# Two of the seven Strassen-Winograd products share one PSUM bank, in both MLP stages of a recurrent decoder layer

## The chip, the core and the metric

The kernel runs on one NeuronCore of a Trainium2 chip. Five engines each run their own instruction stream in order: TensorE (PE, matmuls, with its weight loads shown apart as PEld), VectorE (DVE), ScalarE (ACT), GpSimd (POOL) and SyncE (SP, which here issues most DMA transfers). They wait for each other through semaphores. Matmuls write PSUM, which is divided into banks; DVE and ACT read the sums from there. The metric is the device time of one execution in microseconds (us). The clock granted to TensorE is 2.4 GHz or 1.2 GHz; the profile gives it as a share of full speed.

## What is computed

One inference step of one layer with 2048 prompt tokens and 32 sample tokens (T = 2080). A recurrent mixer comes first and is not touched. What the change touches is the MLP at the end, float32 throughout:

```
h = x * (1.0 + sc2) + sh2
f = jnp.dot(jnp.square(jax.nn.relu(jnp.dot(h, p['mlp_w1']) + p['mlp_b1'])), p['mlp_w2']) + p['mlp_b2']
x = layer_norm(ALPHA * x + g2 * f, p['ln2_g'], p['ln2_b'])
```

`mlp_w1` is 1024 x 4096 and `mlp_w2` 4096 x 1024.

## The kernel before

**Groups and chunks.** The 2080 tokens go through the MLP in three groups, 0, 1 and 2, of 696, 692 and 692 columns (`groups`). A group is two halves of `w` = 348 or 346 columns. Within a group the 4096 hidden features are walked in 16 chunks of 256 (`c`, 0 to 15; 14 in group 2, whose last two chunks take another path). For each chunk `mlp1` makes 256 hidden features for all columns of the group. After four chunks `mlp2_seven` multiplies them by their rows of `mlp_w2` and adds the result to the SBUF tile `acc`. So a group is four times: four calls of `mlp1`, one of `mlp2_seven`.

**Seven products.** Each of these matrix products is cut into 2 x 2 blocks and done with seven block products in Winograd's form instead of eight. With the left operand's combinations a11, a12, a22, s1 to s4 and the right one's b11, b21, b22, t1 to t4:

```
X  = a11*b11            C11 = X + a12*b21
X += s2*t2  (U2)        C12 = U2 + s1*t1 + s4*b22
X += s3*t3  (U3)        C22 = U3 + s1*t1
X += a22*t4             C21 = X
```

s1*t1 is the P5 and s4*b22 the P3 of the title. X is a running sum that stays in one PSUM bank ("the X bank") while a11, s2, s3 and a22 add to it; between two of them an engine reads the bank, and the next product's first matmul has to wait for that read. A product in `mlp1` is 12 matmuls (4 blocks of the contraction, 3 each, since a float32 operand is split in a high and a low part, tiles named h... and l...). In `mlp2_seven` it is 48 matmuls over four banks, two of everything because four chunks make two pairs.

**mlp1 before.** `prod` runs one product, into a new bank from `rot(M1_BANKS, ...)` or onto the one it is given. The reads: s1 <- X after a11 (ACT copy), u2 <- X after s2 (ACT copy), u2 <- X after s3 (ACT copy), and Relu of X after a22 (ACT). The bank of s1*t1, `p5_s`, is read twice by DVE: u4 = p5_s + u2 (U2 + P5), and `put(1, 1, p5_s, u2)` after s3. The product s4 has a bank of its own, which `put(0, 1, ps, u4)` reads. `put` is a DVE instruction that adds bank, bias and an SBUF tile, and then the squared ReLU. Chunk 0 of groups 1 and 2 has an order of its own.

**mlp2_seven before.** `PRODUCTS` lists left operand, right operand, whether the product adds to the X banks, and to which quarters of `acc` its banks are then added. DVE does the adding (`add(V, dst, ps[b], dst)`), ACT a copy where the quarter is still empty. Products not in X take fresh banks from `rot("CD")`.

**Order and weights.** The program is written chunk by chunk, but the compiler's scheduler decides how the instructions of neighbouring chunks interleave on each engine; each engine then runs its list in order. Group 0 makes the combinations of the weights itself (DVE, ACT, POOL), uses them and stores them to `W1d` and `W2d` in HBM. Groups 1 and 2 load them from there, one 512 KB tile for each 12 matmuls, through SP's queue, in the order in which the program names them (`order_of` for mlp1, `PRODUCTS` for mlp2), into 15 slots that are reused in turn (`kept`, `READY`): the load of a tile waits until the tile 15 places earlier has been used.

Matmul results carry the names m1... for `mlp1` and m2... for `mlp2_seven`: the X bank of `mlp1` is m1a11_group_chunk, P5's is m1s1_group_chunk.

Of the kernel before, what the change touches and what calls it, by code (L numbers as in the profile page):

```python
# [12 lines left out]
AF = mybir.ActivationFunctionType  # L13
# [4 lines left out]
P = 128  # L18
# [17 lines left out]
def trunk(ctx: ExitStack, tc: tile.TileContext, *args):  # L36
# [324 lines left out]
    with lpool("ab") as ab:  # L361
# [95 lines left out]
        for nm, rows in (("A", rowsA), ("B", rowsB)):  # L457
            n = sum(r for _, r in rows)
            rt = ab.tile([P, 4, 288], F32, tag="hf", name="rt" + nm, bufs=2)[:, 0, 0:P]
            o = 0  # L460
# [316 lines left out]

    def order_of(gidx, c):

        if c:  # L780
            return "a11", "a12", "s2", "s1", "s3", "s4", "a22"
        return ("a11", "a12", "s4", "s2", "s1", "s3", "a22") if gidx else ("a11", "s2", "s1", "s3", "a22", "a12", "s4")

    def weights(gidx, c):

# [259 lines left out]
    with lpool("p5") as p5_:  # L1045
# [2 lines left out]

        acc = p5_.tile([P, 4, 4, HW], F32, tag="acc", name="acc")

        PRODUCTS = (("a11", "b11", True, (0,)), ("s1", "t1", False, (2, 3)), ("a12", "b21", False, (0,)),
                    ("s2", "t2", True, (2,)), ("s4", "b22", False, (2,)), ("s3", "t3", True, (3,)),
                    ("a22", "t4", True, (1,)))

        def block(q):
            return acc[:, 2 * q:2 * q + 2].rearrange("p a j t -> p (a j) t")
# [1 line left out]
        def mlp1(gidx, c, wts=None):  # L1058
            g0, npr, w = groups[gidx]
            ops = wts or weights(gidx, c)  # L1060
            nm = f"{gidx}_{c}"
            hid = [p5_.tile([P, 2, HW], F32, tag="hid", name=f"hid{q}_{nm}", bufs=8) for q in range(2)]
            hid = [t[:, :, :w] for t in hid]

            def prod(key, rt, o, on=None):

                ps = rot(M1_BANKS, f"m1{key}_{nm}")[:, :w] if on is None else on
                wh, wl = ops[key]
                hh, hl = h2[rt]
                for k in range(4):  # L1070
                    for i, (x, h) in enumerate(((wh, hh), (wh, hl), (wl, hh))):
                        PE.matmul(ps, x[:, k, :], h[:, k, o:o + w], start=(on is None and k + i == 0),  # L1072
                                  stop=(k == 3 and i == 2), skip_group_check=on is not None)
                return ps

            def vt(v):
                return p5r.tile([P, HW], F32, tag="v", name=f"{v}_{nm}", bufs=3)[:, :w]

            def bias(f):
                return vec["mlp_b1"][:, 2 * c + f:2 * c + f + 1]  # L1080

            def square(v, on_act=False):
                if on_act:
                    act(v, v, AF.Relu)
                    act(v, v, AF.Square)
                else:
                    stt(v, v, 0.0, v, ALU.max, ALU.mult)

            def put(f, q, ps, s):
                v = hid[q][:, f, :]  # L1090
                stt(v, ps, bias(f), s, ALU.add, ALU.add)
                square(v, SQA[2 * f + q])

            s1, u2, u4 = vt("s1"), vt("u2"), vt("u4")
            v01, v10 = hid[1][:, 0, :], hid[0][:, 1, :]
            x = p5_s = None
            for key in order_of(gidx, c):
                if key == "a11":
                    x = prod(key, "b1", 0)
                    act(s1, x, AF.Copy)  # L1100
                elif key == "a12":
                    put(0, 0, prod(key, "b2", 0), s1)
                elif key == "s2":
                    prod(key, "t42", w, x)
                    act(u2, x, AF.Copy)
                elif key == "s1":
                    p5_s = prod(key, "t13", 0)
                    add(V, u4, p5_s, u2)
                    if gidx and not c:
                        add(V, v01, v01, u4)  # L1110
                        square(v01, SQA[1])
                elif key == "s3":
                    prod(key, "t13", w, x)
                    act(u2, x, AF.Copy)
                    put(1, 1, p5_s, u2)
                elif key == "s4":
                    ps = prod(key, "b2", w)
                    if gidx and not c:
                        act(v01, ps, AF.Identity, bias=bias(0))
                    else:  # L1120
                        put(0, 1, ps, u4)
                else:
                    prod(key, "t42", 0, x)
                    act(v10, x, AF.Relu, bias=bias(1))
                    act(v10, v10, AF.Square)
            return hid
# [12 lines left out]
        def mlp2_seven(gidx, c0, hids, steps=None):  # L1139
# [44 lines left out]
                        tail(bv, "t4", "b21", "b21", "t2")  # L1184

            taken = [c0 > 0] * 4
            banks = None
            for l, r, grows, to in PRODUCTS:
                rs = []
                for nm, av, bv in pairs:  # L1190
                    prepare(l, nm, av, bv)
                    rs.append(part(f"{r}_{nm}", bv[r]))
                fresh = not (grows and banks)
                if not grows:
                    ps = [rot(M2_BANKS, f"m2{l}_{gidx}_{c0}_{b}")[:, :w] for b in range(4)]
                else:
                    if fresh:
                        banks = [ptile([P, 512], X_BANKS[b], f"m2x_{gidx}_{c0}_{b}")[:, :w] for b in range(4)]
                    ps = banks
                for s_ in range(2):  # L1200
                    for n, ((nm, av, bv), (hh, hl)) in enumerate(zip(pairs, rs)):
                        at = W2d[c0 // 2 + n, KEYS.index(l), s_]
# [139 lines left out]
        BEH = ("s4", "t3", "t4")  # L1342
        SQA = (0, 1, 1, 1)
        PB = 3
        M1_BANKS, M2_BANKS, X_BANKS = "ADB", "CD", "ABAB"
        LATE = range(2, 14, 2)
        STAGE = range(4, 12)
        epst = sel[:, 0, 0:1]
# [537 lines left out]
```

## Time and profile before

| what | value |
|---|---|
| median of 3 runs (lowest, highest) | 2162.76 us (2157.93, 2165.63) |
| the profiled execution, its own time | 2165.93 us |
| its span, first to last instruction | 2164.1 us |
| PE busy / DVE busy / ACT busy | 2038.4 / 1426.8 / 1006.3 us |
| mean granted clock of TensorE | 0.978 |

The profiled execution is 1.8 us longer than its span. The MLP begins near 735 us of the span; group 0 fills most of 780 to 1300 us, groups 1 and 2 follow up to about 2115 us, and the rest is the end of the last layer norm. A share of busy time is an average over these stages, which have different limits, so the rows below are taken stage by stage.

### The profile page before, as it was taken

To read this page: it belongs to the slowest core of one execution; us is meant where nothing else is said; L and a number is where in the kernel's file an instruction comes from. 1 tells how busy PE (TensorE), PEld (TensorE's weight loads), DVE (VectorE), ACT (ScalarE), POOL (GpSimd) and SP (SyncE) were. 2 spreads that over 40 slices of the span, in tenths; PEclk is the share of its full clock that TensorE was granted. 3 is DMA by queue.
4 is the path that set the end of the run, shared out by engine and by line. 5 is a ranking of instruction groups with operands and counts; after the bars stand their busy time and mean duration, and the time that the engine had idled before them with its cause. 6 is when DMAs were issued, how large, how long until landed. Compare 5 with 4: busy or idle time off the path is not lost.

```text
span 2164.1 us, 35479 instructions
## 1 busy us (share of the span) xinstructions
PE 2038.4 (94%) x13055; PEld 1915.4 (89%) x13055; DVE 1426.8 (66%) x2766; ACT 1006.3 (47%) x1923; POOL 489.7 (23%) x327
## 2 busy tenths in 40 slices
PE   7998999989999989889899899999999999999996
PEld 4987888888877789888899889999999999999996
DVE  5677897467887898688797854445444444554476
ACT  3446665546676456554645534333334343333342
POOL 2245323432433322121222401000002000001003
PEclk9999999999999989999999999999999999999998
DMA  9799765453342598999989899888889988898871
GB/s 334 162 267 266 220 192 171 134 149 83 103 110 79 181 325 315 397 341 369 348 325 351 312 365 370 306 282 297 304 293 332 383 302 303 286 310 293 278 271 53
DMA packets 367596, 571.39 MB, mean 264 GB/s; under 512 B 129451, under 2 KB 250703, under 8 KB 367423
## 3 DMA queue, kind: packets, MB, share of 16 engines
q1 hardware_dynamic: 363975, 567.84, 76.8%
q8 instruction: 103, 1.69, 0.3%
q10 hardware_dynamic: 3448, 1.29, 0.2%
q14 instruction: 70, 0.57, 0.1%
HBM read 388.10 MB, written 180.94 MB: 263 GB/s over the span
## 4 chain that ended last, share of the span: by engine, by line
PE 43%; DVE 4%; issue 3%; DMA 2%; POOL 0%; ACT 0%; SPq 0%; POOLq 0%; DVEq 0%; ACTq 0%
PE m1a L1072 15%; PE m2x L1211 11%; PE m1s L1072 6%; PE m2s L1211 6%; PE m2a L1211 3%; PE lt L1297 1%; DVE hw2s L44 1%; DVE acc L44 1%; DMA W1d<-w1s 0%; PE m L1247 0%; PE m L1248 0%; PE m L1249 0%; DVE hid L44 0%; DMA n<-Nd 0%; DVE lb L44 0%
## 5 line engine op out<-in xcount | busy, mean ns | idle before, releaser
L44 POOL TENSOR_TENSOR y<-y,ln_g 128x512 f32<-128x512 f32 (+3 forms) x28 | 37.6, 1360 | 636.7 <-ACT y L65 463.3
L65 ACT ACTIVATE ht<-hid 128x692 fp32r<-128x692 f32 (+1 forms) x92 | 72.1, 783 | 174.1 <-PE m2s L1211 62.8
L65 ACT ACTIVATE hid<-hid 128x346 f32<-128x346 f32 (+1 forms) x240 | 115.9, 491 | 72.3 <-DVE hid L62 63.5
L65 ACT ACTIVATE u<-m1a 128x346 f32<-128x346 f32 (+1 forms) x96 | 43.9, 458 | 188.5 <-PE m1a L1072 181.3
L44 DVE TENSOR_TENSOR lt<-hid,ht 128x692 fp32r<-128x692 f32 (+1 forms) x92 | 87.1, 947 | 64.8 <-ACT ht L65 64.5
L44 DVE TENSOR_TENSOR acc<-m2x,acc 128x346 f32<-128x346 f32 (+1 forms) x168 | 84.3, 513 | 61.4 <-PE m2x L1211 59.9
L62 DVE SCALAR_TENSOR_TENSOR hid<-m1s,vecB,u 128x346 f32<-128x346 f32 (+1 forms) x94 | 53.7, 576 | 97.3 <-ACT u L65 72.6
L44 DVE TENSOR_TENSOR hid<-hid,hid 128x692 f32<-128x692 f32 (+1 forms) x92 | 87.5, 951 | 35.0 <-ACT hid L65 34.9
L1211 PE MATMUL m2x<-ht,hw2s 128*128 128x348 f32 (+1 forms) x392 | 98.9, 329 | 5.3 <-DVE hw2s L44 5.3
L65 ACT ACTIVATE hb<-hid 128x692 fp32r<-128x692 f32 (+1 forms) x69 | 54.0, 784 | 98.7 <-PE m2x L1211 51.6
L44 DVE TENSOR_TENSOR lb<-hid,hb 128x692 fp32r<-128x692 f32 (+1 forms) x69 | 67.2, 974 | 17.6 <-ACT hb L65 17.4
L1211 PEld LDWEIGHTS m2x<-ht,hw2s 128*128 128x128 f32 x392 | 70.3, 194 | 6.6 <-DVE hw2s L44 6.6
L62 DVE SCALAR_TENSOR_TENSOR hid<-m1a,vecB,s 128x346 f32<-128x346 f32 (+1 forms) x48 | 27.6, 576 | 62.5 <-PE m1a L1072 57.5
L44 DVE TENSOR_TENSOR acc<-m2s,acc 128x346 f32<-128x346 f32 (+1 forms) x120 | 56.4, 509 | 13.9 <-PE m2s L1211 13.9
L1211 PE MATMUL m2x<-lt,hw2s 128*128 128x348 f32 (+1 forms) x196 | 63.5, 327 | 0.0
L1072 PE MATMUL m1s<-h2t13h,hw1s 128*128 128x348 f32 (+1 forms) x216 | 57.9, 330 | 4.9 <-DVE x L62 3.7
L44 DVE TENSOR_TENSOR u<-m1s,u 128x346 f32<-128x346 f32 (+1 forms) x48 | 24.8, 516 | 51.9 <-ACT u L65 30.3
L65 ACT ACT_TABLE_LOAD x40 | 51.3, 1283 | 16.0 <-DVE hgb L57 6.5
L1072 PE MATMUL m1a<-h2t42h,hw1a 128*128 128x348 f32 (+1 forms) x192 | 50.9, 328 | 5.8 <-ACT hw1a L65 2.4
L1072 PE MATMUL m1a<-h2t42h,hw1s 128*128 128x348 f32 (+1 forms) x184 | 51.1, 342 | 5.5 <-DVE hw1s L44 4.9
L1072 PE MATMUL m1a<-h2t13h,hw1s 128*128 128x348 f32 (+1 forms) x200 | 52.4, 325 | 2.3 <-ACT hw1s L65 1.7
L956 PE MATMUL op<-hwo,ybh 128*128 128x512 f32 x128 | 51.7, 407 | 2.9 <-ACT ybh L65 2.9
(820 smaller groups left out, 7763.1 us busy)
## 6 DMA issues: line engine op xcount, KB each, us to landing
W1d<-hw1s SPq DMA_DIRECT2D x53, 512.0 KB
W2d<-hw2s SPq DMA_DIRECT2D x53, 512.0 KB
hw1s<-W1d SPq DMA_DIRECT2D x44, 512.0 KB
hw2s<-W2d SPq DMA_DIRECT2D x44, 512.0 KB
lw1s<-W1d SPq DMA_DIRECT2D x42, 512.0 KB
w1s<-W1d SPq DMA_DIRECT2D x42, 512.0 KB
W2d<-hw2a SPq DMA_DIRECT2D x41, 512.0 KB
W1d<-hw1a SPq DMA_DIRECT2D x38, 512.0 KB
```

What stands on the lines that cost most here:

```text
L44: return eng.tensor_tensor(out=out, in0=in0, in1=in1, op=op)
L62: return V.scalar_tensor_tensor(out, in0, s, in1, op0, op1)
L65: return S.activation(out, in_, f, **kw).ins
L956: PE.matmul(ac[:w, :], yh[:, kk, o:o + w], wh[:, hs], start=(k == 0), stop=False)
L1072: PE.matmul(ps, x[:, k, :], h[:, k, o:o + w], start=(on is None and k + i == 0), stop=(k == 3 and i == 2), skip_group_check=on is not None)
L1211: PE.matmul(ps[2 * s_ + jj], x[:, f, js], h[:, f, :], start=(fresh and n + f + e == 0), stop=(n == len(pairs) - 1 and f + e == 3), skip_gr ...
L1297: PE.transpose(pt[:w, k * P:k * P + P], src[:, 4 * half + k, :], ident)
```

## The change

In `mlp1` the product s4 no longer gets a bank of its own: it is added onto the bank `p5_s` of s1, after `put(1, 1, p5_s, u3)` has read P5 alone. Then `put(0, 1, ps, u2)` adds U2 to P5 + P3 in one step, and the DVE instruction that made u4 goes. U3's copy gets a tile u3 of its own, since u2 has to live until then. The order becomes a11, s2, s1, s3, a22, a12, s4 for all chunks except chunk 0 of groups 1 and 2. In `mlp2_seven` the bank sets are named o, x and y; s1 and s4 share set y, s1 is added to quarter 3 alone, and s4 (now P5 + P3) to quarter 2. The order becomes a12, a11, s1, s2, s4, s3, a22.

```
-        if c:
-            return "a11", "a12", "s2", "s1", "s3", "s4", "a22"
-        return ("a11", "a12", "s4", "s2", "s1", "s3", "a22") if gidx else ("a11", "s2", "s1", "s3", "a22", "a12", "s4")
+        if gidx and not c:
+            return "a11", "a12", "s4", "s2", "s1", "s3", "a22"
+        return "a11", "s2", "s1", "s3", "a22", "a12", "s4"
...
-        PRODUCTS = (("a11", "b11", True, (0,)), ("s1", "t1", False, (2, 3)), ("a12", "b21", False, (0,)),
-                    ("s2", "t2", True, (2,)), ("s4", "b22", False, (2,)), ("s3", "t3", True, (3,)),
-                    ("a22", "t4", True, (1,)))
+        PRODUCTS = (("a12", "b21", "o", (0,)), ("a11", "b11", "x", (0,)), ("s1", "t1", "y", (3,)),
+                    ("s2", "t2", "x", (2,)), ("s4", "b22", "y", (2,)), ("s3", "t3", "x", (3,)),
+                    ("a22", "t4", "x", (1,)))
...
                     p5_s = prod(key, "t13", 0)
-                    add(V, u4, p5_s, u2)
                     if gidx and not c:
-                        add(V, v01, v01, u4)
+                        add(V, u2, p5_s, u2)
+                        add(V, v01, v01, u2)
                         square(v01, SQA[1])
                 elif key == "s3":
                     prod(key, "t13", w, x)
-                    act(u2, x, AF.Copy)
-                    put(1, 1, p5_s, u2)
+                    act(u3, x, AF.Copy)
+                    put(1, 1, p5_s, u3)
                 elif key == "s4":
-                    ps = prod(key, "b2", w)
+                    ps = prod(key, "b2", w, p5_s)
                     if gidx and not c:
                         act(v01, ps, AF.Identity, bias=bias(0))
                     else:
-                        put(0, 1, ps, u4)
+                        put(0, 1, ps, u2)
...
-                fresh = not (grows and banks)
-                if not grows:
-                    ps = [rot(M2_BANKS, f"m2{l}_{gidx}_{c0}_{b}")[:, :w] for b in range(4)]
-                else:
-                    if fresh:
-                        banks = [ptile([P, 512], X_BANKS[b], f"m2x_{gidx}_{c0}_{b}")[:, :w] for b in range(4)]
-                    ps = banks
+                fresh = total not in banks
+                if fresh:
+                    banks[total] = [ptile([P, 512], (X_BANKS if total == "x" else M2_BANKS)[b],
+                                          f"m2{total}_{gidx}_{c0}_{b}")[:, :w] for b in range(4)]
+                ps = banks[total]
```

**Place 1, PE, group 1, chunk 7, the end of `mlp1`.** The X bank of this chunk is m1a11_1_7; products on it with h2t13 are s3, those with h2t42 and a22 in the weight's name are a22. Before, s3 ends and matmuls of `mlp2_seven` (m2x) follow:

```order
L1072 MATMUL m1a11_1_7_15208<-h2t13h1_13128,lw1s3_1_7_15197 128x346 x2
L1072 MATMUL m1a11_1_7_15208<-h2t13l1_13129,lw1s3_1_7_15197 128x346
L1072 MATMUL m1a11_1_7_15208<-h2t13h1_13128,lw1s3_1_7_15197 128x346
L1211 MATMUL m2x_1_4_0_15318<-lb11_1_6_15315,hw2a110_1_6_15336 128x346
L1211 MATMUL m2x_1_4_0_15318<-hb11_1_6_15314,hw2a110_1_6_15336 128x346 x2
L1211 MATMUL m2x_1_4_0_15318<-lb11_1_6_15315,hw2a110_1_6_15336 128x346
```

There are 23 matmuls on other banks before a22 goes on with m1a11_1_7. In the changed kernel a22 is the next instruction after s3, and s4 onto the bank of s1 is the next after a22:

```order
L1072 MATMUL m1a11_1_7_15124<-h2t13h1_13072,w1s3_1_7_15111 128x346 x2
L1072 MATMUL m1a11_1_7_15124<-h2t13l1_13073,w1s3_1_7_15111 128x346
L1072 MATMUL m1a11_1_7_15124<-h2t13h1_13072,w1s3_1_7_15111 128x346
L1072 MATMUL m1a11_1_7_15124<-h2t42h1_13074,lw1a22_1_7_15113 128x346
L1072 MATMUL m1a11_1_7_15124<-h2t42l1_13075,lw1a22_1_7_15113 128x346
...
L1072 MATMUL m1a11_1_7_15124<-h2t42h1_13074,lw1a22_1_7_15113 128x346
L1072 MATMUL m1s1_1_7_15151<-h2b2h1_13070,lw1s4_1_7_15117 128x346
```

No matmul is left between s3 and a22 of this chunk, and 12 between s3 and s4.

**Place 2, PE, group 0, chunk 7, the start of `mlp1`.** Products with h2b1 are a11, those with h2b2 a12 and with h2t42 (weight s2) s2. Before, a12 into its own bank stands between and around a11 and s2:

```order
L1072 MATMUL m1a11_0_7_10528<-h2b1l0_8509,hw1a11_0_7_10491 128x348
L1072 MATMUL m1a11_0_7_10528<-h2b1h0_8508,hw1a11_0_7_10491 128x348
L1072 MATMUL m1a12_0_7_10542<-h2b2h0_8844,hw1a12_0_7_10495 128x348 x2
...
L1072 MATMUL m1s1_0_7_10570<-h2t13h0_8510,w1s1_0_7_10505 128x348
L1072 MATMUL m1s1_0_7_10570<-h2t13l0_8511,w1s1_0_7_10505 128x348
L1072 MATMUL m1a11_0_7_10528<-h2t42h0_8512,hw1s2_0_7_10501 128x348
```

Now s2 is the next instruction after a11:

```order
L1072 MATMUL m1a11_0_7_10506<-h2b1h0_8508,hw1a11_0_7_10469 128x348 x2
L1072 MATMUL m1a11_0_7_10506<-h2b1l0_8509,hw1a11_0_7_10469 128x348
L1072 MATMUL m1a11_0_7_10506<-h2b1h0_8508,hw1a11_0_7_10469 128x348
L1072 MATMUL m1a11_0_7_10506<-h2t42h0_8512,hw1s2_0_7_10475 128x348
L1072 MATMUL m1a11_0_7_10506<-h2t42l0_8513,hw1s2_0_7_10475 128x348
```

The 12 matmuls that stood between the two products on the X bank are gone.

**Place 3, SP, the weight loads of chunk 7 in group 1.** Before:

```order
L756 DMA lw1a11_1_7_15189<-W1d_71 128x1024
L756 DMA w1a12_1_7_15191<-W1d_71 128x1024
L756 DMA lw1s2_1_7_15193<-W1d_71 128x1024
L756 DMA w1s1_1_7_15195<-W1d_71 128x1024
L756 DMA lw1s3_1_7_15197<-W1d_71 128x1024
L756 DMA w1s4_1_7_15199<-W1d_71 128x1024
L756 DMA lw1a22_1_7_15201<-W1d_71 128x1024
```

In the changed kernel a12 comes sixth, while on PE it still runs before s2, s3 and a22 of its chunk:

```order
L756 DMA lw1a11_1_7_15105<-W1d_71 128x1024
L756 DMA w1s2_1_7_15107<-W1d_71 128x1024
L756 DMA lw1s1_1_7_15109<-W1d_71 128x1024
L756 DMA w1s3_1_7_15111<-W1d_71 128x1024
L756 DMA lw1a22_1_7_15113<-W1d_71 128x1024
L756 DMA w1a12_1_7_15115<-W1d_71 128x1024
L756 DMA lw1s4_1_7_15117<-W1d_71 128x1024
```

So the loads no longer come in the order of use.

## Rows read from the trace of the kernel before

**Rows 1.** The page's head and its first part: span, busy time of each engine.
```profile
span 2164.1 us, 35479 instructions
PE 2038.4 (94%) x13055; PEld 1915.4 (89%) x13055; DVE 1426.8 (66%) x2766; ACT 1006.3 (47%) x1923; POOL 489.7 (23%) x327
```

**Rows 2.** Windows: length; PE, PEld, DVE, ACT, POOL busy (count); clock; DMA share; GB/s.
```profile
780.00:1300.00 520.00, 477.39 (x2814) 456.82 (x2815) 407.94 (x597) 260.47 (x478) 121.43 (x80) 0.97 0.93 346
1300.00:2100.00 800.00, 799.58 (x5061) 797.73 (x5060) 392.05 (x764) 292.60 (x560) 75.57 (x56) 1.00 0.88 311
```

**Rows 3.** PE's waits, 1300 to 2100 us: total us, times, longest.
```profile
PE lt L1297 <- DVE y L62: 0.4, 1, 0.4
```

**Rows 4.** PE and ACT in order of time, group 0: start, us, instruction, [idle before <-releaser].
```profile
1026.44 0.32 PE L1072 MATMUL m1a<-h2t13h,w1s 128*128 128x348 f32 x1
1026.85 0.46 ACT L65 ACTIVATE u<-m1a 128x348 f32<-128x348 f32 x1 [0.54 <-PE m1a L1072]
1027.37 0.42 PE L1072 MATMUL m1a<-h2t42h,hw1a 128*128 128x348 f32 x1 [0.61 <-ACT u L65]
1027.63 0.32 PE L1072 MATMUL m1a<-h2t42l,hw1a 128*128 128x348 f32 x1
```

**Rows 5.** PE in order of time, the start of group 1.
```profile
1283.21 0.42 PE L1072 MATMUL m1a<-h2t42h,lw1a 128*128 128x346 f32 x1 [0.55 <-ACT u L65]
```

**Rows 6.** The page's costliest groups: DVE instructions the change removes some of; `put`.
```profile
L44 DVE TENSOR_TENSOR acc<-m2x,acc 128x346 f32<-128x346 f32 (+1 forms) x168 | 84.3, 513 | 61.4 <-PE m2x L1211 59.9
L62 DVE SCALAR_TENSOR_TENSOR hid<-m1s,vecB,u 128x346 f32<-128x346 f32 (+1 forms) x94 | 53.7, 576 | 97.3 <-ACT u L65 72.6
...
L44 DVE TENSOR_TENSOR acc<-m2s,acc 128x346 f32<-128x346 f32 (+1 forms) x120 | 56.4, 509 | 13.9 <-PE m2s L1211 13.9
...
L44 DVE TENSOR_TENSOR u<-m1s,u 128x346 f32<-128x346 f32 (+1 forms) x48 | 24.8, 516 | 51.9 <-ACT u L65 30.3
```

**Rows 7.** PE's waits for weights that DVE makes, 735 to 1300 us.
```profile
PE m2s L1211 <- DVE hw2s L44: 7.7, 5, 2.4
...
PE m1a L1072 <- DVE hw1s L44: 5.3, 4, 2.4
PE m2x L1211 <- DVE hw2s L44: 5.3, 4, 3.9
...
PE m1a L1072 <- DVE hw1a L44: 2.3, 3, 1.0
...
PE m2x L1211 <- DVE hw2a L44: 1.8, 2, 1.3
```

**Rows 8.** Busy time in four stretches of group 0, columns as in rows 2.
```profile
880.00:900.00 20.00, 16.96 (x94) 16.31 (x94) 10.12 (x16) 8.75 (x17) 2.65 (x2) 0.91 1.04 411
900.00:920.00 20.00, 17.86 (x107) 16.57 (x106) 16.11 (x25) 13.12 (x26) 4.54 (x3) 1.00 1.00 380
1200.00:1220.00 20.00, 16.17 (x91) 15.59 (x90) 18.76 (x26) 9.25 (x15) 7.28 (x5) 0.91 0.91 352
1220.00:1240.00 20.00, 15.90 (x81) 15.32 (x80) 18.55 (x18) 8.49 (x14) 13.90 (x7) 0.83 0.78 282
```

**Rows 9.** PE in order of time, the last mlp2_seven of group 0: waits for weights.
```profile
1208.20 0.59 PE L1211 MATMUL m2s<-ht,hw2s 128*128 128x348 f32 x2 [1.43 <-DVE hw2s L44]
1212.77 0.95 PE L1211 MATMUL m2s<-ht,hw2s 128*128 128x348 f32 x2 [2.40 <-DVE hw2s L44]
...
1230.33 0.95 PE L1211 MATMUL m2x<-ht,hw2s 128*128 128x348 f32 x2 [3.87 <-DVE hw2s L44]
```

**Rows 10.** SP in order of time: the issue of two 512 KB loads.
```profile
1471.61 0.43 SPq L1286 DMA_DIRECT2D y<-Cd  x1
...
1503.13 0.39 SPq L1286 DMA_DIRECT2D y<-Cd  x1
```

**Rows 11.** ACT in order of time: the two instructions that wait for them.
```profile
1479.02 3.19 ACT L65 ACTIVATE y<-y,AB,mods 128x128 f32<-128x128 f32 x8 [6.94 <-DMA y<-Cd]
...
1508.90 3.20 ACT L65 ACTIVATE y<-y,AB,mods 128x128 f32<-128x128 f32 x8 [3.16 <-DMA y<-Cd]
```

More of the change, by code (lines that the diff above doesn't have):

```diff
@@ L1092, in put @@
                 square(v, SQA[2 * f + q])
-            s1, u2, u4 = vt("s1"), vt("u2"), vt("u4")
+            s1, u2, u3 = vt("s1"), vt("u2"), vt("u3")
             v01, v10 = hid[1][:, 0, :], hid[0][:, 1, :]
@@ L1186, in mlp2_seven @@
             taken = [c0 > 0] * 4
-            banks = None
-            for l, r, grows, to in PRODUCTS:
+            banks = {}
+            for l, r, total, to in PRODUCTS:
                 rs = []
@@ L1344, in trunk @@
         PB = 3
-        M1_BANKS, M2_BANKS, X_BANKS = "ADB", "CD", "ABAB"
+        M1_BANKS, M2_BANKS, X_BANKS = "ADB", "CDCD", "ABAB"
         LATE = range(2, 14, 2)
```

## The prediction

> **What bounds the kernel now.** The page's head comes first: PE is busy 94% of the span and DVE 66% [rows 1]. Such a mean says little, so I cut the span at the borders of the groups [rows 2]. In groups 1 and 2 PE is busy 799.6 of 800 us, the granted clock is full, and it issues 5061 matmuls, one per 0.158 us. The list of PE's waits agrees: 0.4 us in all that stretch [rows 3]. DVE is at 49% there, so a DVE instruction less shortens nothing, and a wait that PE gets is added to the time in full. In group 0 it is otherwise. PE issues 2814 matmuls in 520 us; at 0.158 us they would take 445, so 75 us are lost, while DVE is busy 408 us (78%) and the DMA engines 93%. Three resources are near their end at once there, and relief of one can give something back.
>
> **What the change takes away.** By the order of both kernels the count of matmuls is the same, and so is ACT's; DVE has 94 instructions less. 46 of the 48 that make u4 go (chunk 0 of groups 1 and 2 keeps its one) and 48 of the 336 adds into `acc` (four for each of the twelve calls of `mlp2_seven`). They take 0.516 us and about 0.51 us each [rows 6], together 48 us of DVE. 32 us of them lie in groups 1 and 2, behind a PE that never waits for DVE: worth nothing. 32 instructions, 16.4 us, lie in group 0. There PE waits 22.4 us for weights that DVE has yet to make [rows 7]. The 16.4 us are 4% of DVE's work in that stage, and DVE paces only part of it; DMA at 93% paces the rest. Bounds: nothing, if DMA sets the pace, and 16.4 us, if DVE does all through. I take 4 us, about a quarter, since the waits for DVE are 22.4 of 75 us lost.
>
> **What it adds: reads of a bank with no work between.** Between two products on the X bank of `mlp1` PE waits for an ACT copy of the bank. What hides that is other matmuls in between. Before, a12 stood between a11 and s2, and s4 between s3 and a22; now a12 is sixth, and s4 must itself wait for `put(1, 1)`. I counted in both orders how many matmuls of other banks stand between. In groups 1 and 2 before: at least 12 at each place but two, 0 and 8, mostly 23 or more. After: no matmul at all at 14 places, two at 2, and 6 to 24 or more at the others (place 1 of the change is one of the 14).
>
> The price of no cover is in the trace, since group 0 has the pattern already [rows 4]. The last matmul of s3 starts at 1026.44, the copy runs from 1026.85, a22 starts at 1027.37 and its second matmul at 1027.63. From first to last start 1.19 us pass, where two steps of 0.158 would do: 0.87 us lost. With two matmuls in between 0.32 us less, 0.55; with six, 0.95 us, nothing is left to pay. That is also why the 8 to 23 of before cost none [rows 3].
>
> Of the 14, 11 lie in the middle of groups 1 and 2, where PE has no slack: 11 x 0.87 = 9.6 us. The two places with two matmuls: 1.1 us. The other three are in chunks 0 and 1 of group 1, where before has one such wait, 0.55 us idle [rows 5]: two more, 1.7 us. Sum 12.4 us. Bounds: 10.7 if the start of group 1 is still short of other things and hides its three; upwards ACT's queue, since a copy can stand behind another instruction of its own length, 0.46 us [rows 4], which at 13 places would be 6 us more. ACT is busy 293 of 800 us there [rows 2] and the copy shown started after an idle 0.54 us, so I take none.
>
> In group 0 I count 12 places with no cover and 11 with two, against 4 and 1 before: 8 x 0.87 + 10 x 0.55 = 12.5 us (place 2 is one). But PE waits there for weights in any case, and those are made by others meanwhile: what PE loses before such a wait, the wait gives back. Bounds 0 and 12.5; I take a third, 4 us. It cancels the gain on DVE.
>
> s4 behind `put(1, 1)`: after s3 come the copy (0.46 us) and a DVE instruction of 0.576 us [rows 4, 6]; in every chunk of groups 1 and 2 in the plain order at least 12 matmuls, 1.9 us, stand between s3 and s4, and the stall before a22 lengthens that. Nothing, unless DVE is late by a microsecond; behind the waiting s4 on PE stand the first matmuls of the next product, so a late one would cost in full.
>
> In `mlp2_seven` a bank is read by adds of 0.51 us [rows 6], and the order keeps at least 16 matmuls, 2.5 us, of other banks between two products on one bank (14 before). Nothing.
>
> **What it moves: the loads.** In groups 1 and 2 a weight slot is free for the next load once PE is through with its old tile. By both orders and the 15 slots I counted the matmuls from that release to the first use of the new tile, SP's order observed. Before, the shortest is 72 (11.4 us), after it is 49, and 21 loads have 62 or less: 7.7 to 9.8 us. The cause is place 3: s2, s3, a22 and s4 of a chunk are held until after products of the next one. A 512 KB load takes from issue to use 7.4 us (1471.61 to 1479.02) or 5.8 us (1503.13 to 1508.90) [rows 10, 11]. So 7.7 us is just enough. Bounds: nothing, and 21 loads late by 1 us, 21 us. I take 1 us, since 7.4 is the longer of the two.
>
> The Trainium skill, page "DMA: Bandwidth & Descriptors", section "Anatomy of one DMA", puts a transfer at 2.0 us plus its bytes at 436 GB/s; my estimate from it for 512 KB is 3.2 us, and by it no load would be late and this term 0. The trace shows about twice that here, with the queues shared, so I go by the trace.
>
> **The sum.** 2165.9 (own time of the profiled execution) + 12.4 + 4 - 4 + 1 = 2179. That execution was 3.2 us above the median of the three runs, 2162.8; against the median the same 13.4 us give 2176.
>
> **Rivals.** *Loads come late (slower still).* For it: 7.4 against 7.7 us, a DMA share of 0.88 [rows 2], and a queue in which one late release holds the rest. Against it: after a hold the queue is empty, and the first load then lands sooner. Half of 21 loads late by 2 us: + 21, 2197.
>
> *The clock falls at the new gaps (slower still).* 880 to 900 us has the clock at 0.91, with 16.96 us busy [rows 8]; a mean of 0.91 of two levels, 1 and a half, costs 0.09 x 20 = 1.8 us. Eleven such: + 20, 2196. Against it: 900 to 920 has PE idle for over 2 us in all and a clock of 1.00, and a wait of 0.61 us is less than those around 0.91 and 0.83 (1.43 to 3.87 us [rows 9]). The Trainium skill, page "TensorE: Matmul & The Clock Gate", section "A second HAM failure mode: psum-queue depth-cycling", tells of a kernel whose clock went up and down because of short idle times between groups of matmuls. By that rule this rival would come true; the row of 900 to 920 us speaks against it.
>
> *Group 0 gives more back (faster).* In its last `mlp2_seven` PE stands 1.43, 2.40 and 3.87 us for DVE's weights [rows 9], and the clock at 0.91 and 0.83 costs 1.8 + 3.4 us [rows 8]: 12.9 us in one place. If DVE's lighter list takes these away and the other waits for DVE, 22.4 - 7.7 = 14.7 us, as well, group 0 gives back 27.6 instead of 4: 12.4 + 4 + 1 - 27.6 = -10, 2153. For it: DVE is busy 18.8 and 18.6 of 20 us there [rows 8]. Against it: the weights' own combinations are as many as before, and 8 us of adds less in four calls of `mlp2_seven` are less than the waits they would have to end. It is faster by over 6.5 us only from 24 us given back on.
>
> *It evens out (same).* Group 0 gives back 11 to 24 us; DVE's whole 16.4 would do: 12.4 + 4 + 1 - 16.4 = +1, 2164. It is the bound of the term on DVE, and nothing but the DMA's share speaks against it.
>
> **How the numbers follow.** About 0.3%, 6.5 us, is what a measurement of this kernel can tell from no change. Forecast, 2169 to 2186: 0.52. Loads late 0.10 and clock lower 0.04, above 2186. Same, 2156 to 2169: 0.21. Faster, below 2156: 0.13. So slower 0.66, same 0.21, faster 0.13. The range 2159 to 2193 leaves out about one in ten on either side; with cases of both signs in it, the forecast's own range stands beside it, 2169 to 2186.
>
> **What the profile would show.** Right: in groups 1 and 2 some 13 waits of PE for "ACT u" of 0.5 to 0.7 us at a full clock, about 7 us of idle time and the span of these groups longer by about 12; DVE's busy time down by 48 us; no waits of PE for DMA; group 0 as long as before within 5 us. Wrong: group 0 shorter by over 10 us; PE waiting for W1d or W2d; a clock below 1.00 after 1300 us; or the copies' waits absent, if PE gets past them.

## The result and the profile after

The changed kernel takes 2184.23 us (median of 4 runs, 2183.01 to 2186.61), the kernel before 2160.97 us beside it on the same chip. The ratio is 1.0111, with a 95% interval from 1.0093 to 1.0129: slower by 23 us. The forecast was 2176 us, slower, with 2159 to 2193 as the range.

The profiled execution took 2186.61 us, 20.7 more than that of before. The head and the first part of its page, beside [rows 1]:

```profile
span 2184.8 us, 35303 instructions
PE 2043.1 (94%) x13055; PEld 1915.6 (88%) x13055; DVE 1389.2 (64%) x2672; ACT 1011.9 (46%) x1923; POOL 503.1 (23%) x327
```

DVE has 94 instructions less and is busy 37.6 us less. PE has as many matmuls and is busy about as long, so nearly all of the 20.7 us is time in which PE stands or runs slowly. The same windows as in [rows 2], in the same columns:

```profile
780.00:1300.00 520.00, 467.47 (x2750) 443.70 (x2751) 387.12 (x557) 262.39 (x471) 134.53 (x79) 0.98 0.91 340
1300.00:2100.00 800.00, 794.44 (x5013) 790.12 (x5012) 360.44 (x695) 289.46 (x555) 77.34 (x56) 1.00 0.87 308
```

From 1300 to 2100 us PE was busy for all but 0.4 us; now 5.6 us are idle, at a full clock still, and 48 matmuls less are issued in the same 800 us. Group 0's window has 64 less. PE's waits in the list (us in total, times, longest), 1300 to 2140 us, where before had one of 0.4 us [rows 3]:

```profile
PE m1a L1072 <- ACT u L65: 9.4, 13, 3.2
```

Those are, one by one, the 11 places with no cover and the two with two matmuls that the prediction had counted in the middle and at the end of groups 1 and 2. The first of them is place 1 of the change, chunk 7 of group 1. In order of time (start, us, engine, instruction, [idle before <-releaser]):

```profile
1437.87 0.32 PE L1072 MATMUL m1a<-h2t13h,w1s 128*128 128x346 f32 x1
1438.22 0.46 ACT L65 ACTIVATE u<-m1a 128x346 f32<-128x346 f32 x1 [2.70 <-PE m1a L1072]
...
1438.73 0.42 PE L1072 MATMUL m1a<-h2t42h,lw1a 128*128 128x346 f32 x1 [0.55 <-ACT u L65]
...
1438.99 0.32 PE L1072 MATMUL m1a<-h2t42l,lw1a 128*128 128x346 f32 x1
```

Matmul starts at 1437.87, 1438.73 and 1438.99: 1.12 us for two steps of 0.158, so 0.80 us lost, by the same chain as in [rows 4]: last matmul of s3, ACT's copy, first matmul of a22.

To see where the time went, each kernel's matmul records are counted: the 4600th comes just before the MLP, the 8000th soon after group 1 has begun, the 12500th near the end of group 2. Windows from zero, narrowed until they hold that many, give the moments. Of the changed kernel:

```profile
0.00:729.20 729.20, 674.55 (x4599) 586.08 (x4600) 548.54 (x1227) 408.00 (x802) 251.32 (x164) 0.97 0.61 174
0.00:1353.30 1353.30, 1239.46 (x8000) 1118.48 (x8001) 1000.23 (x1899) 721.45 (x1367) 408.85 (x257) 0.97 0.75 249
0.00:2072.70 2072.70, 1953.30 (x12499) 1828.06 (x12500) 1315.13 (x2494) 973.73 (x1855) 480.52 (x309) 0.98 0.79 268
```

Of the kernel before:

```profile
0.00:732.30 732.30, 675.70 (x4600) 585.54 (x4601) 542.75 (x1227) 407.80 (x802) 254.53 (x164) 0.97 0.61 173
0.00:1347.20 1347.20, 1240.32 (x8000) 1121.14 (x8001) 1010.01 (x1933) 716.59 (x1372) 397.73 (x257) 0.97 0.75 250
0.00:2058.90 2058.90, 1951.59 (x12500) 1830.63 (x12501) 1350.97 (x2582) 968.48 (x1855) 467.27 (x309) 0.98 0.79 270
```

So group 0 with the start of group 1 went from 614.9 to 624.1 us (+9.2), groups 1 and 2 from 711.7 to 719.4 (+7.7), the end from 107.0 to 113.9 (+6.9), and what lies ahead of the MLP, which is not touched, gave 3.1 back. A count to the 7500th matmul splits group 0 from the start of group 1: from the 4600th to it are 532.8 and 535.4 us in two profiles of the kernel before and 539.6 and 540.3 in two of the changed one, so of the 8.2 us between their means at the 8000th some 5.9 lie in group 0 itself.

The end has an event of its own. ACT in order of time:

```profile
2107.83 0.63 ACT L65 ACTIVATE hw<-rw 128x512 fp32r<-128x512 f32 x1
2112.58 0.63 ACT L65 ACTIVATE hw<-rw 128x512 fp32r<-128x512 f32 x1 [4.12 <-DMA rw<-in_mlp_w_dram]
2113.78 0.63 ACT L65 ACTIVATE w<-rw 128x512 fp32r<-128x512 f32 x1 [0.57 <-DMA rw<-in_mlp_w_dram]
2114.32 0.44 ACT L65 ACTIVATE u<-m1a 128x346 f32<-128x346 f32 x1
```

In chunk 14 of group 2 the copy u, for which a22 waits, stands in ACT's list behind splits of weights whose loads land late, and ACT stands 4.12 us. PE waits 3.18 us there (at 2114.81), and behind that wait its clock falls:

```profile
2110.00:2115.00 5.00, 1.82 (x12) 1.54 (x11) 1.64 (x3) 1.61 (x3) 0.02 (x1) 0.90 0.78 284
2115.00:2120.00 5.00, 5.00 (x18) 5.00 (x19) 1.85 (x5) 2.54 (x6) 0.00 (x0) 0.50 0.01 3
2120.00:2125.00 5.00, 4.31 (x25) 4.02 (x24) 2.52 (x4) 3.66 (x8) 1.29 (x1) 0.92 0.00 0
```

0.50 is the lower level, 1.2 GHz: PE is busy all 5 us and issues 18 matmuls, where 33 come in 5 us at full clock.

### The profile page after: what moved, and what is told of

Same layout as the page of the kernel before. It is cut to its first block, busy times and chain, and to the rows that moved or that the text cites. A ratio compares the mean times of both kernels' runs of the same rounds, so it can differ in the third digit from the quotient of the medians.

```text
span 2184.8 us, 35303 instructions
## 1 busy us (share of the span) xinstructions
PE 2043.1 (94%) x13055; PEld 1915.6 (88%) x13055; DVE 1389.2 (64%) x2672; ACT 1011.9 (46%) x1923; POOL 503.1 (23%) x327
## 4 chain that ended last, share of the span: by engine, by line
PE 58%; DVE 19%; DMA 9%; issue 6%; ACT 5%; POOL 2%; SPq 1%; ACTq 0%; DVEq 0%; POOLq 0%
PE m1a L1072 18%; PE m2x L1210 12%; PE m1s L1072 7%; PE m2y L1210 6%; PE m2o L1210 3%; DVE xc L62 2%; PE pa L184 1%; DVE hw2s L44 1%; DVE acc L44 1%; PE accg L372 1%; PE accg L373 1%; PE accg L374 1%; DVE gi L346 1%; PE op L956 1%; PE accb L373 1%
## 5 line engine op out<-in xcount | busy, mean ns | idle before, releaser
L65 ACT ACTIVATE hb<-hid 128x692 fp32r<-128x692 f32 (+1 forms) x69 | 52.8, 780 | 66.0 <-PE m2x L1210 35.3
L1072 PE MATMUL m1s<-h2t13h,hw1s 128*128 128x348 f32 (+1 forms) x192 | 52.6, 334 | 8.4 <-DVE x L62 3.6
L1072 PE MATMUL m1s<-h2b2h,hw1s 128*128 128x348 f32 (+1 forms) x192 | 52.4, 336 | 6.7 <-ACT hw1s L65 3.3
L65 ACT ACTIVATE hid<-m1a,vecB 128x346 f32<-128x346 f32 (+1 forms) x48 | 26.4, 551 | 57.0 <-PE m1a L1072 56.7
L44 DVE TENSOR_TENSOR acc<-m2y,acc 128x346 f32<-128x346 f32 (+1 forms) x84 | 41.7, 511 | 17.4 <-PE m2y L1210 17.4
L957 PE MATMUL op<-hwo,ybl 128*128 128x512 f32 x128 | 51.9, 407 | 0.4 <-DVE ybl L44 0.4
```

What stands on the lines that cost most here:

```text
L44: return eng.tensor_tensor(out=out, in0=in0, in1=in1, op=op)
L65: return S.activation(out, in_, f, **kw).ins
L957: PE.matmul(ac[:w, :], yl[:, kk, o:o + w], wh[:, hs], start=False, stop=False)
```

## The experiments

**Theory.** The loss is made of places where a product stands right behind another one on the bank of `mlp1` that ACT must read first; each costs 0.8 to 0.9 us, in group 0 too. **Rivals.** The new order of `mlp2_seven` costs; the shared bank costs by itself; slots that are held longer make loads late; or group 0's share is chance.

All kernels are the changed kernel with three switches: `new1` (is `mlp1` of this chunk in the changed form and order), `new2` (the same for `mlp2_seven`) and `own22` (does a22 get a bank of its own, to which DVE adds U3):

```
+        if c and not new1(gidx, c):
+            return "a11", "a12", "s2", "s1", "s3", "s4", "a22"
...
+            for l, r, total, to in PRODUCTS if new2(gidx, c0) else OLD:
...
+                elif own22(gidx, c):
+                    put(1, 0, prod(key, "t42", 0), u3)
```

The measurements of all runs stand in one table. "Places" counts group 0's places in `mlp1` with no matmul / with two between products on the X bank. The next three columns are stretches of the profiled execution in us: 4600th to 8000th matmul, 8000th to 12500th, 12500th to the end of its own time. "Half clock" is an estimate of what the lower clock took from 735 to 1335 us: 5-us windows, each 5 us times (1 - granted clock), summed. It is an upper bound, since PE also stands in some of that time. The last column is the ratio to the kernel before on the same chip, with its interval.

| kernel | places | group 0 | groups 1, 2 | end | half clock | ratio to before |
|---|---|---|---|---|---|---|
| before | 4/1 | 614.9 | 711.7 | 107.0 | 17.0 | 1 |
| before again | 4/1 | 617.5 | 711.6 | 107.8 | 15.3 | (one run) |
| changed | 12/11 | 624.1 | 719.4 | 113.9 | 15.3 | 1.0111 (1.0093-1.0129) |
| changed again | 12/11 | 624.7 | 719.7 | 111.4 | 18.9 | (one run) |
| mlp2_seven alone | 2/1 | 610.4 | 718.2 | 109.0 | 8.5 | 1.0049 (1.0033-1.0066) |
| the same, a11 first | 4/2 | 609.3 | 710.6 | 106.9 | 8.5 | 0.9982 (0.9969-0.9995) |
| mlp1 alone | 11/10 | 621.5 | 712.8 | 108.6 | 13.6 | 1.0052 (1.0037-1.0067) |
| group 0 old | 4/1 | 617.3 | 722.0 | 112.3 | 17.0 | 1.0076 (1.0062-1.0090) |
| group 0 alone new | 12/11 | 621.3 | 714.6 | 112.4 | 11.9 | 1.0080 (1.0067-1.0094) |
| a22 in its own bank | 4/6 | 614.1 | 722.6 | 108.8 | 10.2 | 1.0055 (1.0041-1.0069) |
| the same, a12 second | 0/1 | 603.3 | 720.2 | 110.9 | 11.9 | 1.0022 (1.0008-1.0036) |
| last two chunks old | 12/11 | 627.0 | 719.5 | 109.2 | 18.8 | 1.0089 (1.0074-1.0103) |
| group 0 covered | 0/1 | 608.2 | 710.7 | 107.7 | 17.1 | 0.9972 (0.9962-0.9982) |
| group 0 uncovered | 12/11 | 620.9 | 712.5 | 110.4 | 11.9 | 1.0061 (1.0048-1.0074) |

Two cautions. Half clock in group 0 differs between executions of one order (11.9 and 17.1, or 11.9 to 18.9), and so do its lengths; so group 0's column is compared with half clock taken off as well: 598 and 602 before and 600 in the run with group 0 old, 606 to 609 in the five profiles with 12/11 that have the new `mlp2_seven` there, 591.4 and 591.1 with 0/1. And executions of the kernel before ran from 2154 to 2170 us on one chip; both of its profiles, 2165.93 and 2165.06, lie 4 to 7 us above its medians of 2159 to 2161, so where a kernel's own profile lies at its median, its difference to the profile of before is lower than the ratio says by about that much. What made them longer isn't settled.

**Only mlp2_seven changed** (`new1` False everywhere, `new2` True).

> Only the second stage is changed (mlp2_seven with the total y in banks C and D and its new order); mlp1 keeps the old order and its separate add for u4. Theory (the loss is PE standing before a read of its X bank with no other matmuls in between, in mlp1): the order has one such place in groups 1 and 2, as before, so 0 to +3 us against before, and the list of PE's waits after 1300 us shows one wait for ACT u, not thirteen. Rival 1 (the order of mlp2_seven costs, by weights that are needed sooner in group 0): group 0 longer by 5 to 10 us, +5 to +10 in all. Rival 2 (32 fewer adds into acc relieve DVE in group 0): 4 us or more shorter, -4 or below.

2171.08 against 2161.22 us: rival 1's number, but not where it puts it. Group 0 is not longer. The time is lost behind it, by 6.5 us, in waits of another kind:

```profile
PE m2o L1233 <- ACT hb L65: 5.0, 3, 2.0
PE m1a L1086 <- ACT u L65: 1.6, 1, 1.6
PE m2o L1233 <- ACT hid L65: 0.6, 1, 0.6
```

The new `mlp2_seven` begins with a12 times b21, and b21 is what the old `mlp1` makes last; the new `mlp1` makes it two products earlier. The split hb of b21, its high part, is then what PE waits for. A run below tests that.

**Only mlp1 changed** (`new1` True, `new2` False).

> Only the first stage is changed (mlp1 with P5 and P3 in one bank and its new order); mlp2_seven is the old one. Theory: the order has 4 or 5 places without cover in groups 1 and 2 (the old mlp2_seven stands in other places between the chunks), at 0.87 us about 4 us, and all those of group 0; if group 0's 10 us come from these places too, +12 to +16 us in all, group 0 about +10 of it. Rival 1 (group 0 loses by the order of mlp2_seven): +3 to +6 in all, group 0 within 3 us of before. Rival 2 (the shared bank itself is slow, wherever it is used): +16 or more, with idle time in groups 1 and 2 as in the whole change.

2172.17 us, +11 by medians, just below the theory's band. Group 0 is 5 us longer than the mean of before's two profiles (about 8 with half clock taken off), groups 1 and 2 only 1.1: the list has four waits for ACT u, 2.3 us in all, two of them in that stretch. So the shared bank is not slow wherever it is used (rival 2): those two places are worth 1.6 us, and nothing is left for the places with cover.

**Group 0 old, groups 1 and 2 new** (`new1` and `new2` are `gidx > 0`), and **group 0 alone new** (`gidx == 0`).

> Group 0 has the old order in both stages, groups 1 and 2 the new one. Theory: the whole change costs about 10 us in group 0 and 11 to 13 after it, and the two are independent, so +10 to +14 us; the stretch to 1300 us as long as before within 3 us, and about 13 waits of PE for ACT u behind it. Rival 1 (the lateness of group 0 is what makes the rest late, by loads that come behind it): 0 to +6. Rival 2 (groups 1 and 2 carry all, and what group 0 loses is later made up): +18 to +23.

> The counterpart: group 0 has the new order in both stages, groups 1 and 2 the old one. Theory: about +8 to +12 us, all of it before 1320 us, and two waits for ACT u or fewer behind it. Rival 1 (a loss in group 0 is later made up, since the loads of groups 1 and 2 get ahead meanwhile): 0 to +4. Rival 2 (all +20 come from group 0's lateness): +18 or more.

2178.56 and 2177.34 us, +17 and +16: both above the theory's bands (+10 to +14, +8 to +12) and below the +18 of the rivals. In the first, group 0 is as before and the rest has the change's loss: groups 1 and 2 take 10.3 us more with 13 waits for ACT u, the end 5.3. In the second, group 0 is the changed one and groups 1 and 2 lose 2.9, of which one wait of 2.0 us on its own issue, with the clock at 0.66 in the 5 us behind it. So each part is lost without the other. That they simply add is not shown: the halves add up to 33 where the whole is 23; both have a late copy in the end (waits of 2.31 and 3.41 us), counted twice so, which is some 5 of the 10. The rest is not settled.

**mlp2_seven alone, beginning with a11.** Only the first two rows of its list are exchanged against the first run:

```
-        PRODUCTS = (("a12", "b21", "o", (0,)), ("a11", "b11", "x", (0,)), ("s1", "t1", "y", (3,)),
+        PRODUCTS = (("a11", "b11", "x", (0,)), ("a12", "b21", "o", (0,)), ("s1", "t1", "y", (3,)),
```

> As the run with only mlp2_seven changed, but its list begins with a11 and has a12 second: a11, a12, s1, s2, s4, s3, a22, so the right operand of its first product, b11, is one that the old mlp1 makes early, not b21, which it makes last. Theory: what that run lost was PE's wait for the split of b21 (ACT hb, four waits of 0.6 to 2.0 us in groups 1 and 2, and their like in group 0), an effect of pairing the new second stage with the old first; without it 0 to +3 us against before, and no wait for ACT hb of over 0.3 us after 1330 us. Rival (sharing the banks in mlp2_seven costs by itself): +8 to +11 as in that run. Rival 2 (24 adds less in groups 1 and 2 and 24 less in all of DVE pay off): -3 or below.

2156.6 against 2159.33 us, faster by 0.18%: below the theory's 0 to +3, and by the ratio (some 4 us) at rival 2's -3 or below. No wait for hb is left; in 1350 to 2140 us the list names a single wait, in the last layer norm. So the wait for b21 was the whole loss of the first run behind group 0, and sharing a bank set in `mlp2_seven` is free. What its 48 adds less bring is these few us at most; 1.1 of them show in groups 1 and 2.

**a22 in a bank of its own, a12 still sixth** (`own22` True but in chunk 0 of groups 1 and 2), and **the same with a12 second** (order a11, a12, s2, s1, s3, a22, s4).

> As the change, in its order (a12 sixth), but a22 in a bank of its own with one put more for each chunk. By the order of the matmuls groups 1 and 2 lose all their places without cover but two at the start of group 1; group 0 keeps 4 with none and 6 with two (the change: 12 and 11). Theory: 9 places less in groups 1 and 2, 8 us, the end of group 2 shorter by 3 to 6 us, and of group 0's 10 us about half given back, so -14 to -18 us against the change, +5 to +9 against before. Rival (group 0's loss is of another kind): -9 to -12 against the change, +11 to +14 against before.

> The whole change with P5 and P3 in one bank in both stages, but no product of mlp1 stands right behind another on the X bank: a22 gets a bank of its own, to which DVE adds U3 (one more put for each chunk), and the order is a11, a12, s2, s1, s3, a22, s4 for every chunk after the first. By the order of the matmuls one place without cover is left in groups 1 and 2 beside the one that before had, and none in group 0 (one with two matmuls). Theory (the uncovered reads are the loss, in group 0 too): -2 to +4 us against before; the list of PE's waits has two or fewer for ACT u after 1330 us. Rival (group 0's 10 us come from the shared bank or from DVE's other order, not from the uncovered reads): +8 to +12, in the stretch to 1320 us. Rival 2 (slots held longer): waits for W1d or W2d in groups 1 and 2, +5 or more.

2171.55 and 2164.57 us, +12 and +5 against 2159.33. Group 0 behaved as the theory has it: with 4/6 places it is 10 us shorter than in the change, with 0/1 21 (2 to 5, and 14 to 17, with half clock off). The order of these is that of the places, the sizes are not in proportion to them: from 0/1 to 4/6 it is 12.5 us with half clock off for places worth 6.2, and from 0/1 to the 4/1 of before 7 to 11 us for places worth 3.5, so the order of the products has a second effect in group 0, which was not separated. Groups 1 and 2 did not follow: 722.6 and 720.2 us, longer than in the change. The second kernel's waits there:

```profile
PE m1s L1086 <- DVE hid L62: 3.6, 4, 1.2
PE m1a L1086 <- ACT u L65: 2.2, 2, 1.6
...
PE m1s L1086 <- ACT u L65: 1.7, 1, 1.7
PE m2o L1233 <- ACT hb L65: 1.6, 4, 0.4
PE m2o L1233 <- ACT u L65: 0.9, 2, 0.5
```

With a22 gone from the X bank, the scheduler put s4 close behind s3 in four chunks, and now s4 waits for `put(1, 1)` on the shared bank, which is ACT's copy and then DVE: 1.16 us twice where no matmul is between, 0.70 and 0.53 with three and four. In the first kernel all four have none, 4.7 us. One uncovered read had been exchanged for a longer one. With it, the first products of `mlp2_seven` wait for hb and u as well. By their totals both kernels miss the theory: the first has +12 where 5 to 9 was expected, which is the rival's number (+11 to +14), though group 0 moved as the theory says; the second has +5 where -2 to +4 was expected, with five waits for ACT u instead of two or fewer. PE's waits between the 8000th and the 12500th matmul come to 7.5 and 6.7 us, with some 0.3 us of steps beside each, where the theory had next to none.

**The last two chunks of group 2 in the old mlp1** (`new1` is `not (gidx == 2 and c >= NCK - 2)`).

> The change everywhere but in mlp1 of chunks 14 and 15 of group 2 (the last two), which have the old order and the separate u4. It takes away the wait of 3.18 us for the copy u in chunk 14 and the fall of the clock behind it (0.50 in 2115 to 2120 us). Theory (that wait, half the clock for 5 us, and the two waits behind it are worth 4 to 7 us): -4 to -7 us against the change, +16 to +19 against before; the windows of the last 100 us show a clock of 1.00 up to the end of chunk 15. Rival (PE waits at that place for the same late split in any order, as it waits 3.41 us in the run with group 0 alone changed): within 2 us of the change, and a wait of 2 us or more near 2110 us.

2179.18 us; by the two ratios 5 us less than the change, though their intervals overlap, and the end 109.2 instead of 113.9 and 111.4. ACT still stands 3.46 us for the load of a split and the copy u still comes late, at 2114.50; but 25 matmuls now stand between s3 and a22 of chunk 14, and PE does not wait there. One wait of 1.05 us comes later, ahead of a22 of chunk 15, which has two matmuls of cover. The clock stays up:

```profile
2110.00:2115.00 5.00, 5.00 (x34) 5.00 (x33) 1.76 (x3) 3.04 (x6) 0.85 (x1) 1.00 0.20 83
2115.00:2120.00 5.00, 4.90 (x30) 4.45 (x29) 3.90 (x6) 3.42 (x8) 1.74 (x2) 1.00 0.00 0
2120.00:2125.00 5.00, 3.86 (x20) 3.45 (x21) 4.07 (x5) 4.97 (x12) 1.30 (x1) 1.00 0.00 0
```

**Both kernels once more, for a second profile.**

> The kernel before once more, for a second profile of its group 0, since the first was taken of an execution 5 us above the median. If group 0's 10 us are real, its 8000th matmul comes at 1305 to 1314 us; if the first profile was an unusually short group 0, at 1318 us or later.

> The changed kernel once more, for the same reason. Theory: its 8000th matmul at 1318 to 1325 us, 8 us or more behind the kernel before, and the wait of over 2 us for the copy u near 2110 us with half the clock behind it is there again. Rival (group 0's loss was the luck of one execution): within 4 us of the kernel before at the 8000th matmul.

The counts in these two expectations were made with windows whose borders count a matmul twice, so 8000 there is nearer to 7800; the table has the comparison with exact counts: 617.5 against 624.7 us. That is 7.2 us, just short of the theory's 8 and clear of the rival's 4. The wait in the end came again, shorter than the 2 us expected, as 1.79 us, with clocks of 0.84 in the 5 us that hold it and 0.82 in the next 5.

**Group 0 covered or not, all else in one order.** Groups 1 and 2 have the old `mlp1` and `mlp2_seven` with a11 first; group 0 has P5 and P3 in one bank, once with a22 in its own bank and a12 second, once as in the change:

```
+    def new1(gidx, c):
+        return gidx == 0
...
+            for l, r, total, to in (PRODUCTS[1], PRODUCTS[0], *PRODUCTS[2:]) if gidx else PRODUCTS:
```

> The best parts together. Group 0 as in the run with a22 in its own bank and a12 second (P5 and P3 in one bank, no place without cover, one with two matmuls); groups 1 and 2 have the old mlp1 and the mlp2_seven that begins with a11. Theory: from the 4600th matmul to the 8000th 603 to 608 us (before: 614.9 and 617.5), the rest as before, so 2148 to 2156 us, -4 to -12 us against before. Rival (group 0's gain was the luck of one execution): as the run with the old mlp1 and a11 first in all groups, -1 to -5 us, 609 us or more in that stretch.

> The same kernel, groups 1 and 2 in the same order of products, but group 0's mlp1 in the order of the change (12 places without cover and 11 with two matmuls, against none and one). It prices the places of group 0 by themselves, beside the run before it on the same chip. Theory (full price, 0.87 us for none and 0.55 for two: 12 x 0.87 + 10 x 0.55 = 16 us): +14 to +20 us against that run. Rival (what the prediction assumed, that two thirds are given back in waits for weights that come later): +4 to +7. Rival 2 (nothing to do with the places): within 3 us.

2153.23 and 2172.73 us on one chip, before 2159.42. The covered one has the lowest ratio of all, 0.28% faster than before, though its interval overlaps that of the run with a11 first; its group 0, 608.2 us, lies at the edge of what the theory gave, but with half clock off it is 591.1, as in the earlier run. The uncovered one is 19.5 us behind it: 12.7 in group 0 (17.9 with half clock off), 4.5 behind it, where a wait of 1.64 us and three short ones came, and 2.3 ahead of the MLP, where the two kernels are the same. Full price was 16; the total lies in the theory's +14 to +20 only with the 6.8 us from elsewhere, while group 0 alone is between the theory and the rival's +7. PE's waits, 780 to 1280 us, covered:

```profile
PE m2y L1233 <- DVE hw2s L44: 9.2, 3, 7.4
PE m1a L1086 <- DMA hw1s<-W1d: 4.1, 1, 4.1
...
PE m1a L1086 <- ACT u L65: 0.7, 1, 0.7
```

and uncovered:

```profile
PE m2y L1233 <- DVE hw2s L44: 9.5, 6, 4.4
...
PE m1a L1086 <- ACT u L65: 4.9, 13, 0.6
...
PE m1a L1086 <- ACT s L65: 3.3, 7, 0.9
```

Up to 1275 us the copies' waits go from 0.9 us (2) to 8.2 (20), and each of the 18 more has, as in the timeline above, some 0.3 us of steps beside its wait: 13 us. All waits for weights go from 39.6 to 34.8. But 4.3 of the 39.6 are loads from W1d at the start of group 1, which the uncovered kernel has not reached by 1275 us; the waits for the weights of group 0 itself go from 35.3 to 34.8, and with the stretch from 735 us on from 37.8 to 34.8. So group 0 gives back 0.5 to 3 us of the 13. Counted from the 4600th matmul to the 7500th, ahead of those loads, the uncovered kernel takes 15.1 us more (536.8 against 521.7), to the 8000th 12.7: the start of group 1 gives 2.4 back. What makes up the rest of the 15.1, the list of waits doesn't tell; the two kernels also differ in the order of a12 and in a22's bank, and half clock takes 5.2 us less in the uncovered one.

## Why the prediction was right, point by point

**The side and the mechanism were right.** PE runs in order and stands at each uncovered read; the places counted in the order are the places in the trace, 13 of 13 behind the start of group 1.

**Groups 1 and 2, the price of a place: right.** From the 8000th to the 12500th matmul lie nine places without cover and two with two matmuls; at 0.87 and 0.55 they come to 8.9 us. The two profiles of each kernel give 7.7 to 8.1. The place shown above lost 0.80, so the price was a tenth too high. ACT's queue was taken at nothing, and in these eleven the wait was never over 0.55 us.

**The end: the bound came true, not the value.** The last two places, chunks 14 and 15 of group 2, were counted with 0.87 each, 1.7 us. The end grew by 3.6 to 6.9. The text named ACT's queue as the upward bound, with another instruction of 0.46 us ahead of the copy; what stood there was a split that itself waited 4 us for a load, and then the clock fell. The run with the last two chunks in the old order took 2 to 5 us of the end back. So a fall of the clock, the rival's event, came at this one place, though at one long wait and not at the short ones the rival meant. At the eleven waits of up to 0.55 us it did not: the row of 1300 to 2100 us has 1.00. The Trainium skill's page "TensorE: Matmul & The Clock Gate", section "A second HAM failure mode: psum-queue depth-cycling", tells of short and frequent idle times between groups of matmuls at which the clock went up and down; these eleven did not do it. The wait of 3.18 us came with 0.90 and then 0.50, that of 1.79 us with 0.84 and 0.82. The length of the wait does not settle it: in the run with mlp2_seven alone two waits of 1.98 us left the clock at 1.00, here the first of them:

```profile
1865.00:1870.00 5.00, 3.73 (x23) 3.68 (x24) 3.47 (x5) 2.53 (x4) 0.00 (x0) 1.00 0.88 314
```

What else decides it stays open.

**Group 0, the price: the step that failed.** "what PE loses before such a wait, the wait gives back", said the text of PE's waits for weights, and so of 12.5 us a third was taken. The waits show that at most two fifths come back, not two thirds. Between covered and uncovered, 13 us of stalls are added and 0.5 to 3 us of waits for group 0's weights are gone. Between before and the change, 780 to 1275 us, the copies' waits grow from 1.8 (3) to 8.2 (20), with their steps 11.5 us more; before:

```profile
PE m1a L1072 <- ACT u L65: 1.8, 3, 0.6
```

and after:

```profile
PE m1a L1072 <- ACT u L65: 4.9, 13, 0.6
...
PE m1a L1072 <- ACT s L65: 3.3, 7, 0.9
```

The waits for weights fall by 2.4 us in one pair of profiles and 4.6 in the other. The copies' stalls alone are near the 12.5 us of the prediction's full price; what failed is the share of it that was taken to come back.

**Group 0, DVE's relief: not seen, beside what the clock may owe to it.** 4 us were taken. With half clock off, group 0 with the old `mlp1` is 598 to 602 us with the old `mlp2_seven` and 601 to 602 with the new one: nothing to within 2 us, the lower bound. The 6 to 7 us by which these runs look shorter in the table are the clock's, 8.5 against 17.0 and 15.3; whether a lighter DVE kept the clock up there, or chance did, is open. By its ratio the kernel with a11 first gains 1 to 7 us in all, 1.2 of them behind group 0. DVE's busy time fell by 37.6 in one pair of profiles and by 45.7 in the other, near the 48.

**The sum in group 0.** Forecast were 4 - 4, for the start of group 1 1.7, and at most the 1 for loads: 2.7 us. Measured: 624.4 less 616.2, means of two profiles, 8.2, of which 5.9 by the 7500th matmul, where the sum had nothing, and 2.3 behind it, near the 2.7. The 5.5 us too little, with 2 to 5 at the end and 1 too much in groups 1 and 2, are what lies between 2176 and 2184. These misses mostly add up; the forecast did not come right by one of them making up for another.

**s4 behind put(1, 1): right.** With 12 matmuls or more in between no wait for hid in any profile of the change behind 1300 us. What it costs without them, the runs with a22 in its own bank show: 1.16 us of waiting.

**Loads: right.** None of the 21 loads with 49 to 62 matmuls of lead was late. At the start of group 1 one profile of the change has waits of 1.42 and 1.90 us for W1d, the other none of these; the two kernels with 0/1, whose last product of group 0 comes at 1248 and 1255 us instead of 1274 in the change, wait 3.8 and 4.1 us for one load there. So the start of group 1 can take back part of what group 0 gains, a term that the prediction did not have. The 3.2 us that the prediction works out from the Trainium skill's page "DMA: Bandwidth & Descriptors", section "Anatomy of one DMA", rest on a fit that the section gives for transfers issued from GpSimd; these loads go through SP's queue.

**The rivals.** Loads, clock as a whole, group 0 giving back, evening out: none. Two of the signs named for being wrong did show, each in one place: a clock below 1.00 after 1300 us, at the end, and PE waiting for W1d, in one profile at the start of group 1. The whole change is made slower by the order of `mlp1`; that of `mlp2_seven` alone is free where it begins with an operand that is made early.

## What to carry to other kernels

Where an engine that runs in order is the bound, count in the order of the program what stands between a write to a PSUM bank, the read of it and the next write; each place without cover costs the round trip in full (here 0.8 us), and a stage with other waits gives only part of it back (here two fifths at most). An order that removes an addition from an engine with slack can cost more on the one that has none. Two stages that feed each other are ordered together: one that begins with what the other makes last waits for it.

## What the runs showed that was not expected

The time that group 0 spends at half clock changes from one execution to the next by more than what was looked for: 11.9 and 17.1 us with one order, 11.9 to 18.9 with another. With it taken off, the length of group 0 in the profiles of these two orders differs by 0.3 and 3.6 us instead of 4.9 and 6.1 (in those of the old order by 4.3 instead of 2.6, so it is not the whole scatter). A difference of 5 us in that stage, read from one profile of each kernel, says nothing.
